# The output projection of an attention layer summed in PSUM by column blocks, most of it after the attention, with half a weight chunk per attention step

## The chip, the cores and the metric

The kernel runs on one core of a Trainium2 chip. The metric is device microseconds of one execution. TensorE (PE) multiplies, VectorE (DVE) and ScalarE (ACT) do everything elementwise, GpSimd (POOL) and SyncE (SP) start transfers. [...]

## The reference

One encoder layer on 256 tokens of width 2048: adaptive modulation from a condition vector `c`, windowed attention with a sink logit per head, and a squared-ReLU MLP. All in fp32.

```python
mod = silu(c) @ mod_w + mod_b                 # 2048 x 12288
sh_m, sc_m, g_m, sh_f, sc_f, g_f = split(mod, 6)
h = x * (1 + sc_m) + sh_m
q, k, v = split(h @ w_qkv + b_qkv)            # 32 query heads, 8 key heads of 64; rotary on q and k
m = max(max(s), sink);  p = exp(s - m);  p = p / (sum(p) + exp(sink - m))
y = (p @ v) @ w_o + b_o                       # 2048 x 2048
x = layer_norm(alpha * x + (1 + g_m) * y)
h = x * (1 + sc_f) + sh_f
y = square(relu(h @ w1 + b1)) @ w2 + b2       # 2048 x 8192 x 2048
x = layer_norm(alpha * x + (1 + g_f) * y)
```

## The kernel before

**Weights.** `Stream` loads every weight in chunks of 128x2048 fp32 (1 MB) on SP into one of five buffers `raw` (eight at the start). A matmul operand is split in two parts that the fast fp32 form of PE takes exactly: ACT writes the high part `wh` (L382), DVE the remainder `wl` (L351), each in halves of 128x1024, five buffers each. A product is three matmuls (`mm3`, L685 to L687): high by high, high by low, low by high. I call 12 such matmuls, all that one half of a chunk feeds for 256 tokens in the projections, a **half**; a chunk is two halves.

**Modulation.** A modulation chunk is computed in one of two ways. In the row form (`Mod.step`, L458) PE multiplies it by the condition vector; in the column form (`Col.step`, L498) DVE does, in one pass over 128x2048. The gate of the attention, `m_gm`, has eight chunks of the row form and eight of the column form (`GMP = 1`); the groups `m_ff[0]` and `m_ff[1]` for the MLP have four and four each (`FFP`). `Gate.spread` makes the gate vector a row for all partitions: PE transposes it, ACT copies it out (`grow`, L599), POOL writes it to memory (`rowm`, L600) and reads it back twice, once for each half of the columns, to all partitions (L602).

**Order.** The first part (to about 125 us) multiplies by most of w_qkv in an order that a planner makes. Seven chunks of w_qkv stay (`LATE`). Two of them run before the first scores. Then a loop over `n` interleaves 16 attention steps with one whole weight chunk a step: steps 0 to 4 take the last five chunks of w_qkv, and from `n = OUT_AT = 5` on there are 16 chunks of w_o, in the order of `OUTS`, four column blocks `c` for each of the four head groups `j`. Step `n` computes scores of four heads by 128 queries (`scores`: PE L922, then DVE L929 with mask and row minimum, then ACT L939 the exponential), `normalise` (DVE L947 and L951, ACT L954), and for the step before it the transposes of the probabilities (`probs_T`, PE L964, ACT L966); every second step `values` (PE L980) makes the attention output of a head pair, split into `oh` (ACT L983) and `ol` (DVE L984), which `project` multiplies by w_o.

**Sums of the projection.** `project(c, j)` adds up one head group in two PSUM banks and DVE adds them to a sum `ys` in SBUF (L1075 for `j = 0`, with the bias `bo` that a transfer spread over all partitions, and L1077). For `j = 3` `add_gated` (L989 to L991) multiplies by the gate, adds to the residual and takes statistics.

**Who decides the order.** The program names a sequence; a scheduler orders each engine's instructions ahead of time by its own estimate of when an operand is ready, and each engine then runs its list strictly in order. A wait of one instruction therefore holds up everything behind it on its engine. Modulation chunks stand in the stream in front of the weight chunk of their step (`SLOT_FILL` says how many).

After the projection come layer norm, the first MLP part (`W1A`, L1238 to L1240, with the rest of the modulation), and 620 us of dense MLP matmuls (L1264, L1266).

Of the kernel before, what the change touches and what calls it, by code (L numbers as in the profile page):

```python
# [15 lines left out]
OP = mybir.AluOpType  # L16
# [3 lines left out]
D = 2048  # L20
S = 256
NT = S // 128
NK = D // 128
# [27 lines left out]
def mod_chunks():  # L51

    out = []
    for which, sizes, prods in (("m", MIXG, MIXP), ("f", FFG, FFP)):
        k0 = 0
        for nk, p in zip(sizes, prods):
            out += [("w" + which, p, k0, i) for i in range(2 * p)]
            out += [("c" + which, n, k, 0) for k in range(k0 + p, k0 + nk) for n in range(2)]
            k0 += nk
    for which, p in (("m", GMP), ("f", 0)):  # L60
        out += [("rg" + which, h, i, 0) for h in range(p) for i in range(8)]
        out += [("cg" + which, 0, k, 0) for k in range(8 * p, NK)]
    return {c: i for i, c in enumerate(out)}
# [105 lines left out]
def hybrid_kernel(ctx: ExitStack, tc: tile.TileContext, a, out: bass.AP):  # L169
# [9 lines left out]
    def bank(name="pa"):  # L179
        return psum.tile([128, 512], F32, name=name, tag="bank")  # L180
# [92 lines left out]
    def bias_rows(src, n):  # L273
# [16 lines left out]

        def add(ps, c):
            nc.tensor.matmul(ps, sel[:, c * 128:c * 128 + 128], hl, start=False, stop=True)

# [271 lines left out]
    class Gate(Group):  # L565

        def __init__(self, which, p, gb):
            self.row = dram.tile([1, D], F32, name="row" + which)
            rows, cols, self.p, self.gb = [], [], p, gb
            self.ms = []  # L570
            for h in range(p):
                m = Mod([MODS["rg" + which, h, i, 0] for i in range(8)], 256)
                m.out = lambda m=m, h=h: self.rows(m, h)
                self.ms.append(m)
                rows += [(m, i) for i in range(8)]
            self.col = cst.tile([128, NK], F32, name="col" + which)
            cols = [(Col(MODS["cg" + which, 0, k, 0], self.col[:, k:k + 1]), 0)
                    for k in range(8 * p, NK)]
            self.set(rows, cols)

        def rows(self, m, h):
            pt = bank("pt")
            r = sml.tile([128, 256], F32, name="mrow", bufs=1)
            nc.scalar.copy(r, m.ps[:, :256])
            for x in range(2):
                nc.tensor.transpose(pt[:, x * 128:x * 128 + 128], r[:, x * 128:x * 128 + 128], ident)
            v = pt[:, :256].rearrange("p (x j q) -> p j x q", x=2, j=4)[:, :, :, 0]
            d = self.col[:, 8 * h:8 * h + 8].rearrange("p (j x) -> p j x", j=4)
            b = self.gb[:, 8 * h:8 * h + 8].rearrange("p (j x) -> p j x", j=4)
            nc.vector.tensor_tensor(d, v, b, op=OP.add)  # L590

        def spread(self, g):

            d, b = self.col[:, 8 * self.p:], self.gb[:, 8 * self.p:]
            nc.vector.tensor_tensor(d, d, b, op=OP.add)
# [85 lines left out]
    def part(tiles, t, c):  # L681
        return tiles[c][:, t * 512:t * 512 + 512]
# [302 lines left out]

    def add_gated(ps, t, c, gt, stats):
# [35 lines left out]
    def normed(c, t):  # L1022
# [8 lines left out]
        else:  # L1031
            tc.keep_in_program_order(nc.vector.tensor_scalar(z, z, mv[:, 0:1], rstd, op0=OP.subtract, op1=OP.mult))

    def project(c, j):

        pss = [bank() for _ in range(NT)]
        last = j == 3 and c == 3
# [3 lines left out]
        def step(t, rs):  # L1041
            for r in rs:
                s = slice(t * 512 + r * 128, t * 512 + r * 128 + 128)
                mm3(pss[t], oh[:, s], ol[:, s], wh(r), wl(r), r == 0, r == 3)

        if last:
            for t in range(NT):
# [3 lines left out]
                else:  # L1051
# [4 lines left out]
                    S.pump(4)  # L1056
                add_gated(pss[t], t, c, g1, st)
                sc.append(norm_scalars(st[t]))
# [5 lines left out]
        for r in (0, 2):  # L1064
            for t in range(NT):
                step(t, (r, r + 1))
            S.done()
            if r == 0:
                yield
        for t, ps in enumerate(pss):  # L1070
            if j == 0 and t == 0:
                ys[c] = g4b()
            y = part(ys, t, c)
            if j == 0:
                nc.vector.tensor_add(y, ps, bo(c))  # L1075
            elif j < 3:
                nc.vector.tensor_add(y, y, ps)  # L1077
            else:
                add_gated(ps, t, c, g1, st)
        if j == 2:  # L1080
            project_0(c)


    def project_0(c):

        for t in range(NT):
            y, z = part(ys, t, c), part(xs, t, c)
            nc.vector.tensor_mul(y, y, g1(c))
            nc.vector.scalar_tensor_tensor(z, z, ALPHA, y, op0=OP.mult, op1=OP.add)

# [20 lines left out]
    def mids(n):  # L1111
# [5 lines left out]
        return out  # L1117

    todo = []
    S.behind = True  # L1120
    for n in range(OUT_AT + 16):
        j, i = n // 4, n % 4
# [8 lines left out]
        w = iter(())  # L1131
        if n + PRE < len(LATE):
            w = qkv(*LATE[n + PRE])
        elif n >= OUT_AT:
            if n == OUT_AT:
                bo = bias_all(a["bo"], [g4b(), g4b()])
            w = project(*OUTS[n - OUT_AT])
        mid = mids(n)
        if j < 3:
# [16 lines left out]
        if n == 17:  # L1156
            ff_columns(0)


# [251 lines left out]
def _layout(i):  # L1411
# [13 lines left out]
    def chunk(kind, p, k, j):  # L1425
# [6 lines left out]
        if kind[0] == "r":  # L1432
            m = mw[:, g][:, p * 1024:p * 1024 + 1024].reshape(8, 2, 128, 1024)[k]
            return m.transpose(1, 0, 2).reshape(128, 2048)
# [55 lines left out]
```

## Time and profile before

| | us |
|---|---|
| median of 3 runs (lowest, highest) | 1085.61 (1085.3, 1085.9) |
| span of the profiled execution | 1083.7 |
| first scores on PE start | 165.06 |
| last projection matmul starts | 349.16 |
| DMA read and written | 291.68 MB |

The span runs from the first instruction to the last; what lies around it is 1.9 us against the median. The profile gives busy time per engine, groups of equal instructions with their mean duration and the idle time in front of them, timelines, and waits with the instruction that ended them. The start of an instruction is exact; rows of the same engine overlap slightly at their ends, so the distance of two starts is the price of a row in a dense stretch.

### The profile page before, as it was taken

The page shows a single profiled execution, that of the slowest core. Times are in us where ns is not written, and L with a number is a line of the kernel's source. Part 1 is how long each engine was busy: PE and PEld are TensorE (multiplying, and loading weights), DVE is VectorE, ACT ScalarE, POOL GpSimd, SP SyncE. Part 2 cuts the span into 40 slices and gives each one's busy share as a digit, 9 for nine tenths or more (in the row PEclk, how much of TensorE's full clock was granted, in tenths as well). Part 3 has the DMA queues.
Part 4 walks back from the last instruction along what each step waited for, and adds up shares of the span by engine and source line. Part 5 has one row for each costly group of instructions (what it writes and reads, how often), then busy time and mean ns, then how long its engine had stood idle before and what let it go on. Part 6 is the DMA issues. An engine that isn't in the chain of part 4 may idle for free.

```text
span 1083.7 us, 16256 instructions
## 1 busy us (share of the span) xinstructions
PE 1064.7 (98%) x6519; PEld 881.5 (81%) x6519; DVE 785.3 (72%) x1134; ACT 527.5 (49%) x814; POOL 19.7 (2%) x41
## 2 busy tenths in 40 slices
PE   8999999999999999999999999999999999999997
PEld 6777776677777899988888888888888888888885
DVE  3587689798799888754688789656665557665795
ACT  2453348777772646633345443344553334554340
POOL 2000000000000000000000010000000000000000
PEclk9999999999999999999999999999999999999999
DMA  9999997898973997555777889756555555557522
GB/s 380 425 425 425 427 407 270 352 348 344 391 277 122 420 352 273 193 194 194 272 272 274 295 293 319 297 203 222 194 194 188 192 193 201 181 181 263 194 78 78
DMA packets 43692, 292.75 MB, mean 270 GB/s; under 512 B 4916, under 2 KB 5076, under 8 KB 9824
## 3 DMA queue, kind: packets, MB, share of 16 engines
q1 hardware_dynamic: 40256, 281.82, 69.3%
q0 software_dynamic: 2496, 8.43, 2.3%
q10 hardware_dynamic: 864, 1.45, 0.4%
q8 instruction: 51, 0.84, 0.3%
q14 instruction: 25, 0.20, 0.0%
HBM read 289.57 MB, written 2.11 MB: 269 GB/s over the span
## 4 chain that ended last, share of the span: by engine, by line
PE 91%; DVE 5%; DMA 1%; ACT 1%; issue 1%; SPq 0%; DVEq 0%; ACTq 0%
PE pa L685 17%; PE pa L687 17%; PE pa L686 16%; PE pa L1264 16%; PE pa L1266 8%; PE pa L1240 3%; PE pa L1238 3%; PE pa L1239 3%; DVE raw L498 2%; PE pm L458 2%; PE gv L458 1%; PE pa L922 1%; PE pt L964 1%; PE pa L980 1%; DMA raw<-in_mod 1%; DVE wl L351 1%
## 5 line engine op out<-in xcount | busy, mean ns | idle before, releaser
L351 DVE TENSOR_TENSOR wl<-raw,wh 128x1024 fp32r<-128x1024 f32 x332 | 403.7, 1222 | 222.4 <-ACT wh L382 205.6
L382 ACT CAST wh<-raw 128x1024 fp32r<-128x1024 f32 x298 | 311.6, 1052 | 346.3 <-PE pa L687 203.1
L685 PE MATMUL pa<-wh,g 128*128 128x512 f32 x816 | 324.1, 398 | 2.7 <-ACT g L782 1.4
L687 PE MATMUL pa<-wh,g 128*128 128x512 f32 x816 | 319.3, 391 | 0.5 <-DVE g L984 0.4
L686 PE MATMUL pa<-wl,g 128*128 128x512 f32 x816 | 319.0, 391 | 0.5 <-DVE wl L351 0.4
L1264 PE MATMUL pa<-g,wh 128*128 128x512 f32 x768 | 192.3, 392 | 0.0
L685 PEld LDWEIGHTS pa<-wh,g 128*128 128x128 f32 x816 | 153.3, 188 | 42.7 <-issue 8.2
L687 PEld LDWEIGHTS pa<-wh,g 128*128 128x128 f32 x816 | 153.3, 188 | 34.6 <-issue 1.3
L686 PEld LDWEIGHTS pa<-wl,g 128*128 128x128 f32 x816 | 153.5, 188 | 31.4 <-DVE wl L351 1.2
L1264 PEld LDWEIGHTS pa<-g,wh 128*128 128x128 f32 x768 | 138.3, 189 | 25.1 <-ACT wh L382 0.2
L498 DVE CUSTOM_DVE_ANT_0 raw<-raw,cb 128x2048 f32<-128x2048 f32 x52 | 118.5, 2283 | 9.3 <-ACT cb L868 5.6
L1266 PEld LDWEIGHTS pa<-g,wl 128*128 128x128 f32 x768 | 104.8, 190 | 7.5
L1266 PE MATMUL pa<-g,wl 128*128 128x256 f32 x768 | 107.1, 282 | 0.0
L1240 PE MATMUL pa<-g,wl 128*128 128x256 f32 x256 | 72.3, 284 | 1.9 <-DVE wl L351 1.9
L1238 PE MATMUL pa<-g,wh 128*128 128x256 f32 x256 | 72.7, 285 | 0.3 <-ACT g L1173 0.3
L1239 PE MATMUL pa<-g,wh 128*128 128x256 f32 x256 | 72.4, 284 | 0.0
L1240 PEld LDWEIGHTS pa<-g,wl 128*128 128x128 f32 x256 | 48.9, 192 | 2.1 <-DVE wl L351 2.1
L1238 PEld LDWEIGHTS pa<-g,wh 128*128 128x128 f32 x256 | 49.1, 192 | 1.0 <-ACT g L1173 0.6
L1239 PEld LDWEIGHTS pa<-g,wh 128*128 128x128 f32 x256 | 49.1, 192 | 0.4 <-issue 0.4
L393 ACT CAST wh<-raw 128x1024 fp32r<-128x1024 f32 x34 | 34.8, 1048 | 21.8 <-DMA raw<-in_wqkv 19.6
L939 ACT ACTIVATE g<-g,nm 128x256 f32<-128x256 f32 x64 | 31.8, 498 | 13.1 <-DVE nm L929 13.0
L929 DVE CUSTOM_DVE_ANT_0 g<-pa,msk,nsnk 128x256 f32<-128x256 f32 x64 | 27.1, 477 | 6.3 <-PE pa L922 6.3
(204 smaller groups left out, 743.6 us busy)
## 6 DMA issues: line engine op xcount, KB each, us to landing
raw<-in_mod SPq DMA_DIRECT2D x96, 1024.0 KB, 8.8
raw<-in_w SPq DMA_DIRECT2D x64, 1024.0 KB, 4.8
raw<-in_w1b SPq DMA_DIRECT2D x48, 1024.0 KB, 4.8
raw<-in_wqkv SPq DMA_DIRECT2D x24, 1024.0 KB, 15.3
raw<-in_wo SPq DMA_DIRECT2D x16, 1024.0 KB, 7.4
raw<-in_w1a SPq DMA_DIRECT2D x16, 1024.0 KB, 7.4
g<-in_x SPq DMA_DIRECT2D x4, 512.0 KB, 9.1
gb<-in_lnrow POOLq DMA_DIRECT2D x8, 256.0 KB, 5.7
```

Of the source, the lines that this page charges most:

```text
L351: self.pinned(nc.vector.tensor_sub(l, r, f32(self.hs[n])))
L382: self.last[n] = nc.scalar.copy(h, s)
L393: self.pinned(nc.scalar.copy(h, s))
L498: S.pinned(nc.vector.tensor_tensor_reduce(out=raw, in0=raw, in1=cb, scale=1.0, scalar=0.0, op0=OP.mult, op1=OP.add, accum_out=self.dst))
L685: S.pinned(nc.tensor.matmul(ps, xh, wh, start=start, stop=False))
L686: nc.tensor.matmul(ps, xh, wl, start=False, stop=False)
L687: S.prev = nc.tensor.matmul(ps, xl, wh, start=False, stop=stop).ins
L1238: nc.tensor.matmul(o, wh(w, 128), hh, start=new, stop=False)
L1239: nc.tensor.matmul(o, wh(w, 128), hl, start=False, stop=False)
L1240: nc.tensor.matmul(o, wl(w, 128), hh, start=False, stop=end)
L1264: nc.tensor.matmul(ps, wh(k, 128), ff_in(k), start=k == 0, stop=False)
L1266: nc.tensor.matmul(ps[:, :256], wl(k, 128), ff_in(k)[:, :256], start=False, stop=k == NK - 1)
```

## The change

The modulation: `m_gm` gets twelve chunks of the row form and four of the column form (`GMP = 3`, with rows of four chunks in place of eight), `m_ff[0]` and `m_ff[1]` get eight of the column form each and none of the row form. The bytes are the same.

The weights beside the attention: `HALVES` says how many halves a step takes. Attention steps 0 to 16 take one each, step 8 two; the twelve steps behind take two each. `chain` is the one sequence of halves that the steps draw from, so the order of chunks is by sequence, not by step number. Modulation is planned one chunk a step up to the thirteenth step, then none for three steps, and two a step behind the attention.

The projection: the chunks go by column block (`OUTS`), and the two banks of a block stay open over all four head groups (`out_of`). The bias comes as one more matmul a bank (`bo`, through `bias_rows` as for qkv). The sums `ys` in SBUF, the additions and `project_0` go; `add_gated` takes the factor alpha of the residual into its second operation. The gate is spread after step 15 in place of step 11.

```diff
-OUT_AT = 5
-X_AT = 11
-SLOT_FILL = (1, 1, 1, 1, 1, 1, 1, 2, 2, 2, 2, 2, 2, 2, 2, 2, 2, 2, 2, 2, 1, 0, 0)
+HALVES = (2, 2, 1, 1, 1, 1, 1, 1, 1, 1, 2, 1, 1, 1, 1, 1, 1, 1, 1, 2, 2, 2, 2, 2, 2, 2, 2, 2, 2, 2, 2)
+X_AT = 12
+SLOT_FILL = (1, 1, 1, 1, 1, 1, 1, 1, 1, 1, 1, 1, 1, 1, 1, 1, 0, 0, 0, 1, 2, 2, 2, 2, 2, 2, 2, 2, 1, 0, 0)
-FFP = (2, 2, 4, 0)
-GMP = 1
+FFP = (0, 0, 4, 0)
+GMP = 3
...
-    OUTS = [(c, j) for j in range(4) for c in range(4)]
-    for n in range(-PRE, OUT_AT + 16):
+    OUTS = [(0, 0), (0, 1), (0, 2), (1, 0), (0, 3), (1, 1), (1, 2), (1, 3), (2, 0), (2, 1), (2, 2), (2, 3), (3, 0), (3, 1), (3, 2), (3, 3)]
+    halves = taken = 0
+    for n in range(-PRE, len(HALVES) - PRE):
         plan_late(SLOT_FILL[n + PRE])
...
-        if n + PRE < len(LATE):
-            wq(*LATE[n + PRE])
-        elif n >= OUT_AT:
-            S.plan(a["wo"][OUTS[n - OUT_AT]])
+        halves += HALVES[n + PRE]
+        while 2 * taken < halves:
+            v = (LATE + OUTS)[taken]
+            if taken < len(LATE):
+                wq(*v)
+            else:
+                S.plan(a["wo"][v])
+            taken += 1
...
-        nc.vector.tensor_add(z, z, tmp)
+        if scale is None:
+            nc.vector.tensor_add(z, z, tmp)
+        else:
+            nc.vector.scalar_tensor_tensor(z, z, scale, tmp, op0=OP.mult, op1=OP.add)
...
-        pss = [bank() for _ in range(NT)]
+        pss = out_of[c] = out_of.get(c) or banks()
...
-                mm3(pss[t], oh[:, s], ol[:, s], wh(r), wl(r), r == 0, r == 3)
+                mm3(pss[t], oh[:, s], ol[:, s], wh(r), wl(r), j == 0 and r == 0, j == 3 and r == 3)
...
+            if r and j == 0:
+                for t in range(NT):
+                    bo(pss[t], c, False)
...
-        for t, ps in enumerate(pss):
-            if j == 0 and t == 0:
-                ys[c] = g4b()
-            y = part(ys, t, c)
-            if j == 0:
-                nc.vector.tensor_add(y, ps, bo(c))
-            elif j < 3:
-                nc.vector.tensor_add(y, y, ps)
-            else:
-                add_gated(ps, t, c, g1, st)
-        if j == 2:
-            project_0(c)
+        if j == 3:
+            for t in range(NT):
+                add_gated(pss[t], t, c, g1, st, ALPHA)
...
+    def chain():
+        for v in LATE[PRE:]:
+            yield from qkv(*v)
+            yield
+        for v in OUTS:
+            yield from project(*v)
+            yield
...
-        next(w, None)
+        if k:
+            next(work)
+        else:
+            S.pump(2)
         for f in mid:
             f()
-        next(w, None)
+        if k > 1:
+            next(work)
...
-        if n == 11:
+        if n == 7:
+            split_bo, bo = bias_rows(a["bo"], D)
+        if n == 8:
+            split_bo()
+        if n == 15:
             g1 = m_gm.spread([g4(), g4()])
```

The change moves instructions on each engine. Three places show it; in all of them the rows are the lists of one engine, in the order in which it runs them. (Line numbers after the change are up to eleven higher: L498 and L351 stay, L884 to L891 of the rotary positions become L887 to L894, L929 becomes L932, L922 becomes L925, L964 becomes L967, L984 becomes L987, L989 becomes L992.)

DVE, from the second column-form chunk (`colm`, L498) to the first scores (`msk`), before. `trig` marks the rotary positions of a block of queries or keys, `wl` a weight remainder.

```order
L498 ISA raw,colm<-raw,cb 128x2048
L498 ISA colm 128x1
L886 TENSOR_TENSOR g_1463<-g_1354,trig 128x16x32
L889 TENSOR_TENSOR g_1354<-g_1354,trig 128x16x32 x2
L351 TENSOR_TENSOR wl<-raw,wh 128x1024
L891 TENSOR_TENSOR g_1354<-g_1354,g_1463 128x1024
L351 TENSOR_TENSOR wl<-raw,wh 128x1024
L929 ISA g_1545,nm<-pa,msk,nsnk 128x256
```

The same stretch of the changed kernel, from the end of the same rotation on:

```order
L894 TENSOR_TENSOR g_1354<-g_1354,g_1495 128x1024
L351 TENSOR_TENSOR wl<-raw,wh 128x1024 x2
L498 ISA raw,colm<-raw,cb 128x2048
L498 ISA colm 128x1
L787 TENSOR_TENSOR g_657<-g_657,pa 128x512 x2
L889 TENSOR_TENSOR g4b<-g_657,trig 128x16x32 x2
L892 TENSOR_TENSOR g_657<-g_657,trig 128x16x32 x2
L588 TENSOR_TENSOR colm<-pt,pack 128x4
L894 TENSOR_TENSOR g_657<-g_657,g4b 128x1024
L351 TENSOR_TENSOR wl<-raw,wh 128x1024
L498 ISA raw,colm<-raw,cb 128x2048
L932 ISA g_1595,nm<-pa,msk,nsnk 128x256
```

Two more column-form chunks, the addition of a finished qkv block, its whole rotation and one `wl` now stand between that rotation and the first scores.

PE, the changed kernel, from the end of the third late w_qkv chunk. `pt<-ident,g` are transposes, first of the keys and queries (L910), then of the probabilities of step 0 (L967); L925 are the scores of steps 0 and 1, then of 2.

```order
L690 MATMUL pa<-wh,g_1115 128x512
L292 MATMUL pa<-g_127,g_129 128x512 x2
L458 MATMUL pm<-raw,cact 32x128 x16
L585 MATMUL pt<-ident,mrow 128x128
L910 MATMUL pt<-ident,g_1343 128x128 x8
L910 MATMUL pt<-ident,g_1354 128x128 x8
L925 MATMUL pa<-g_1545,g_1576 128x256 x8
L458 MATMUL pm<-raw,cact 32x128 x16
L967 MATMUL pt<-ident,g_1595 128x128 x8
L925 MATMUL pa<-g_1545,g_1576 128x256 x4
L688 MATMUL pa<-wh,g_255 128x512
```

Before, the scores of step 0 stood inside the third late chunk, with seven of its matmuls, the bias and the scores of step 1, and then 15 matmuls of the fourth behind them and ahead of the transposes of step 0; now that chunk stands ahead of the key transposes, and one modulation chunk is all that lies between the scores and the transposes.

DVE, the changed kernel, behind the last scores. L992 is the first operation with the spread gate (`g_2865`); L987 makes the low part `g_2790` of the last `values`.

```order
L351 TENSOR_TENSOR wl<-raw,wh 128x1024
L498 ISA raw,modf<-raw,cb 128x2048
L498 ISA modf 128x1
L992 TENSOR_TENSOR tmp<-pa,g_2865 128x512
L987 TENSOR_TENSOR g_2790<-pa,g_2789 128x512
L996 SCALAR_TENSOR_TENSOR g_2110<-g_2110,tmp 128x512
L498 ISA raw,modf<-raw,cb 128x2048
```

On PE the first user of that low part stands 19 rows behind the last transposes' first row, in the projection of head group 3:

```order
L983 MATMUL pa<-g_2900,g_1365 64x256 x4
L689 MATMUL pa<-wl,g_2154 128x512
L690 MATMUL pa<-wh,g_2155 128x512
L688 MATMUL pa<-wh,g_2154 128x512
L689 MATMUL pa<-wl,g_2154 128x512
L688 MATMUL pa<-wh,g_2789 128x512
L689 MATMUL pa<-wl,g_2789 128x512
L690 MATMUL pa<-wh,g_2155 128x512
L688 MATMUL pa<-wh,g_2154 128x512
L690 MATMUL pa<-wh,g_2790 128x512
```

Before, the first operation with the gate came some 20 us behind the copy `grow`, and the low parts of `values` had no gate operation ahead of them.

More of the change, by code (lines that the diff above doesn't have):

```diff
@@ L60, in mod_chunks @@
     for which, p in (("m", GMP), ("f", 0)):
-        out += [("rg" + which, h, i, 0) for h in range(p) for i in range(8)]
-        out += [("cg" + which, 0, k, 0) for k in range(8 * p, NK)]
+        out += [("rg" + which, h, i, 0) for h in range(p) for i in range(4)]
+        out += [("cg" + which, 0, k, 0) for k in range(4 * p, NK)]
     return {c: i for i, c in enumerate(out)}
@@ L289, in split, with add @@
             nc.scalar.copy(sel, one)
-        def add(ps, c):
-            nc.tensor.matmul(ps, sel[:, c * 128:c * 128 + 128], hl, start=False, stop=True)
+        def add(ps, c, stop=True):
+            nc.tensor.matmul(ps, sel[:, c * 128:c * 128 + 128], hl, start=False, stop=stop)
         return split, add
@@ L571, in __init__ @@
             for h in range(p):
-                m = Mod([MODS["rg" + which, h, i, 0] for i in range(8)], 256)
+                m = Mod([MODS["rg" + which, h, i, 0] for i in range(4)], 128)
                 m.out = lambda m=m, h=h: self.rows(m, h)
                 self.ms.append(m)
-                rows += [(m, i) for i in range(8)]
+                rows += [(m, i) for i in range(4)]
             self.col = cst.tile([128, NK], F32, name="col" + which)
             cols = [(Col(MODS["cg" + which, 0, k, 0], self.col[:, k:k + 1]), 0)
-                    for k in range(8 * p, NK)]
+                    for k in range(4 * p, NK)]
             self.set(rows, cols)
@@ L583, in rows @@
             r = sml.tile([128, 256], F32, name="mrow", bufs=1)
[L584 to L589, printed above, removed]
+            nc.scalar.copy(r[:, :128], m.ps[:, :128])
+            nc.tensor.transpose(pt[:, :128], r[:, :128], ident)
+            v = pt[:, :128].rearrange("p (j q) -> p j q", j=4)[:, :, 0]
+            d, b = (u[:, 4 * h:4 * h + 4] for u in (self.col, self.gb))
             nc.vector.tensor_tensor(d, v, b, op=OP.add)
         def spread(self, g):
-            d, b = self.col[:, 8 * self.p:], self.gb[:, 8 * self.p:]
+            d, b = self.col[:, 4 * self.p:], self.gb[:, 4 * self.p:]
             nc.vector.tensor_tensor(d, d, b, op=OP.add)
@@ L984, in values, with add_gated @@
         return lambda: nc.vector.tensor_sub(ol, po, f32(oh))
-    def add_gated(ps, t, c, gt, stats):
+    def add_gated(ps, t, c, gt, stats, scale=None):
         tmp = sml.tile([128, 512], F32, name="tmp", tag="t2", bufs=3)
@@ L1032, in normed @@
             tc.keep_in_program_order(nc.vector.tensor_scalar(z, z, mv[:, 0:1], rstd, op0=OP.subtract, op1=OP.mult))
+    out_of = {}
     def project(c, j):
-        pss = [bank() for _ in range(NT)]
+        pss = out_of[c] = out_of.get(c) or banks()
         last = j == 3 and c == 3
@@ L1056, in project @@
                     S.pump(4)
-                add_gated(pss[t], t, c, g1, st)
+                add_gated(pss[t], t, c, g1, st, ALPHA)
                 sc.append(norm_scalars(st[t]))
@@ L1069, in project @@
                 yield
-        for t, ps in enumerate(pss):
-            if j == 0 and t == 0:
-                ys[c] = g4b()
-            y = part(ys, t, c)
-            if j == 0:
-                nc.vector.tensor_add(y, ps, bo(c))
-            elif j < 3:
-                nc.vector.tensor_add(y, y, ps)
-            else:
-                add_gated(ps, t, c, g1, st)
-        if j == 2:
-            project_0(c)
[L1084 to L1089, printed above, removed]
+        if j == 3:
+            for t in range(NT):
+                add_gated(pss[t], t, c, g1, st, ALPHA)
     a2 = cst.tile([128, NK], F32, name="a2")
@@ L1117, in mids @@
         return out
+    def chain():
[5 more added lines that the diff above has]
+            yield
     todo = []
+    work = chain()
     S.behind = True
-    for n in range(OUT_AT + 16):
+    S.pace = 1
+    for n in range(len(HALVES) - PRE):
         j, i = n // 4, n % 4
@@ L1130, in hybrid_kernel @@
             late_tiles.append(1)
[L1131 to L1137, printed above, removed]
+        k = HALVES[n + PRE]
         mid = mids(n)
@@ L1432, in chunk @@
         if kind[0] == "r":
-            m = mw[:, g][:, p * 1024:p * 1024 + 1024].reshape(8, 2, 128, 1024)[k]
+            m = mw[:, g][:, p * 512:p * 512 + 512].reshape(4, 4, 128, 512)[k]
             return m.transpose(1, 0, 2).reshape(128, 2048)
```

3 lines of the change are left out of this document (2 added, 1 removed).

## The prediction, made before the changed kernel ran

> **What bounds the kernel now.** I read the page's first part, then a table of windows around the attention, then PE's waits, then timelines.
>
> ```profile
> span 1083.7 us, 16256 instructions
> ...
> PE 1064.7 (98%) x6519; PEld 881.5 (81%) x6519; DVE 785.3 (72%) x1134; ACT 527.5 (49%) x814; POOL 19.7 (2%) x41
> ```
>
> PE is busy for 1064.7 of 1083.7 us. So time goes down only if PE has less to do or waits less, and only 19 us of waiting exist in the whole span. The part that the change touches lies between 120 and 350 us:
>
> ```profile
> core 0: us, PE busy (x) PEld busy (x) DVE busy (x) ACT busy (x) POOL busy (x), PEclk, DMA share, GB/s
> ...
> 120.00:165.00 45.00, 44.49 (x287) 33.70 (x287) 36.44 (x43) 18.31 (x26) 0.64 (x2) 1.00 0.94 393
> 165.00:312.00 147.00, 146.25 (x1083) 105.46 (x1083) 127.43 (x277) 112.05 (x275) 3.15 (x6) 1.00 0.91 347
> 312.00:350.00 38.00, 38.00 (x204) 29.84 (x206) 34.76 (x64) 15.70 (x30) 0.00 (x0) 1.00 0.43 153
> ```
>
> The columns are the stretch, then the busy time of PE, its weight loads, DVE, ACT and POOL, the granted clock, the DMA share and the rate. PE stands still for 0.5, 0.75 and 0.0 us in these three stretches, at full clock. DVE is the next engine (127 of 147 us). The waits of PE in the stretch from 120 to 361 us say which are left:
>
> ```profile
> PE pt L1167 <- ACT g L1030: 1.4, 1, 1.4
> ...
> PE pa L687 <- DVE g L984: 0.4, 1, 0.4
> ...
> PE pt L964 <- ACT g L954: 0.3, 1, 0.3
> ```
>
> The largest (1.4) belongs to the layer norm, which stays. The softmax wait (L964 for the normalised probabilities) costs 0.3 us, once: between scores and transposes PE has enough dense matmuls. The change takes half of these matmuls away from the attention, so what it can gain on PE must stand against waits that are hidden now.
>
> **The change part by part.** The PE prices are distances of starts:
>
> ```profile
> 139.53 0.62 PE L292 MATMUL pa<-g,g 128*128 128x512 f32 x2
> 139.99 0.39 PE L685 MATMUL pa<-wh,g 128*128 128x512 f32 x1
> 140.22 0.39 PE L686 MATMUL pa<-wl,g 128*128 128x512 f32 x1
> ...
> 155.38 1.04 PE L907 MATMUL pt<-ident,g 128*128 128x128 f32 x8
> ...
> 162.73 1.07 PE L458 MATMUL pm<-raw,cact 128*32 128x256 f32 x16
> 163.73 1.09 PE L907 MATMUL pt<-ident,g 128*128 128x128 f32 x8
> ...
> 173.41 0.84 PE L964 MATMUL pt<-ident,g 128*128 128x128 f32 x4 [0.27 <-ACT g L954]
> ```
>
> A dense matmul costs 0.23, a half 12 x 0.227 = 2.72, a pair of bias matmuls 0.46, a row-form modulation chunk 1.0 to 1.1, eight transposes 0.8 to 1.05.
>
> *PE's work.* The row form goes from 8 + 4 + 4 to 12 chunks in these three groups: 4 fewer, -4.4 us. The bias adds eight matmuls, +1.8. One transpose of the modulation goes, -0.1. Sum **-2.7** (-3.2 to -2.2). The two small waits above vanish or are counted below in another form: **-0.7**.
>
> *DVE's work.* Out go 16 additions to `ys`, eight with the bias and sixteen of `project_0`, each under 0.7 us, some 24 us; in come four column-form chunks, 8.8 us.
>
> ```profile
> L382 ACT CAST wh<-raw 128x1024 fp32r<-128x1024 f32 x49 | 50.8, 1048 | 20.4 <-PE pa L687 20.0 <-DMA raw<-in_wqkv 0.2
> ...
> L1077 DVE TENSOR_TENSOR g4b<-g4b,pa 128x512 f32<-128x512 f32 x16 | 10.9, 681 | 3.5 <-PE pa L687 3.5
> ```
>
> I cost this relief at nothing. It lies on an engine that PE never waited for longer than 0.4 us here. Where DVE stands does matter, and that is the next term.
>
> *The first softmax.* Up to 160.58 us DVE's list is the same before and after, so the trace of before gives the start, and prices for what follows:
>
> ```profile
> 146.57 1.29 DVE L889 TENSOR_TENSOR g<-g,trig 128x512 f32<-128x512 f32 x2
> 147.78 1.22 DVE L351 TENSOR_TENSOR wl<-raw,wh 128x1024 fp32r<-128x1024 f32 x1
> ...
> 153.09 1.28 DVE L784 TENSOR_TENSOR g<-g,pa 128x512 f32<-128x512 f32 x2
> ...
> 156.56 2.28 DVE L498 CUSTOM_DVE_ANT_0 raw<-raw,cb 128x2048 f32<-128x2048 f32 x1
> 158.77 0.08 DVE L498 DVE_READ_ACCUMULATOR2_ANT colm<- 128x1 f32 x1
> ...
> 160.58 1.22 DVE L351 TENSOR_TENSOR wl<-raw,wh 128x1024 fp32r<-128x1024 f32 x1
> 161.72 1.22 DVE L891 TENSOR_TENSOR g<-g,g 128x1024 f32<-128x1024 f32 x1
> 162.85 1.22 DVE L351 TENSOR_TENSOR wl<-raw,wh 128x1024 fp32r<-128x1024 f32 x1
> ...
> 166.34 0.48 DVE L929 CUSTOM_DVE_ANT_0 g<-pa,msk,nsnk 128x256 f32<-128x256 f32 x1 [2.27 <-PE pa L922]
> ...
> 167.96 1.22 DVE L351 TENSOR_TENSOR wl<-raw,wh 128x1024 fp32r<-128x1024 f32 x1
> ```
>
> A column-form chunk costs 2.2, a `wl` 1.14, a rotated block 1.13, a pair of 128x512 operations 1.2, four score rows 1.62. Before, DVE was idle for 2.27 us when the first scores came: it was early. Now DVE runs from 160.58: rotation 161.7, two `wl` 164.0, column form 166.2, and the addition pair (its PE sums end with the bias at about 165.2) 167.4, two rotation pairs 169.8, the small one 169.9, last rotation 171.0, `wl` 172.2, column form 174.4. Only then come the scores of step 0, until 176.0; those of step 1 and a `wl` stand ahead of the sum that the normalisation needs, 179.2.
>
> ```profile
> 172.85 1.71 ACT L954 ACTIVATE g<-g,rs 128x256 f32<-128x256 f32 x4 [1.03 <-DVE rs L951]
> ```
>
> ACT normalises until 180.9 and the eight transposes end at about 181.6. PE meanwhile: 36 matmuls, a bias pair and two modulation chunks from 155.38 bring it to 166.3; the transposes of `mrow`, keys and queries to 169.2, scores of steps 0 and 1 to 171.4, one modulation chunk to 172.5. Its next rows are the transposes of step 0, and everything dense stands behind them. It could end them at 173.6 and ends them at 181.6: **+8.0** (7 to 9).
>
> *The clock behind a wait.* After a long wait of PE the trace shows a lower granted clock:
>
> ```profile
> 14.94 1.08 PE L458 MATMUL gv<-raw,cact 128*32 128x128 f32 x32 [2.03 <-DMA raw<-in_mod]
> ...
> 16.00:18.00 2.00, 2.00 (x9) 1.42 (x6) 0.16 (x1) 0.00 (x0) 0.00 (x0) 0.62 1.02 418
> 18.00:20.00 2.00, 2.00 (x34) 1.38 (x32) 0.00 (x0) 0.00 (x0) 0.00 (x0) 0.53 1.02 422
> ```
>
> Two windows at 0.62 and 0.53 lose 0.76 + 0.94 = 1.7 us. I take **+1.7** after the first softmax (0 if the clock holds, 3.4 if it falls twice). [...]
>
> *The later attention steps.* Beside them PE loses 15 halves (17 in place of 32) and about six modulation chunks: 146.25 - 41 - 6 = 99 us. ACT loses 15 `wh` of 1.0: 112.05 - 15 = 97. So PE and ACT now have nearly equal work, and the chain from scores over softmax to transposes gets half the cover that it had. PE takes one score group ahead, so most of the chain should hide; I take **+2** of 0 to 10. The upper end is 16 steps with some 0.6 us each uncovered; the row of 0.3 above is nearer to the low end.
>
> *The gate row.* `Gate.spread` moves from step 11 to step 15, and DVE's first use of it (L992) now stands ahead of L987, whose low part PE needs 19 rows behind the last transposes. From the copy `grow` PE has about 34 dense matmuls, eight transposes and eight `values` matmuls to do, 7.7 + 0.8 + 1.0, less the 0.5 of the copy: about 9 us until it needs L987. How long the row takes is shown twice, beside weight loads and in the MLP:
>
> ```profile
> 280.87 0.25 ACT L599 COPY grow<-pt 16x128 f32<-16x128 f32 x1
> ...
> 286.82 1.08 POOL L602 DMA_DIRECT2D g<-rowm  x2 [4.91 <-DMA rowm<-grow]
> ...
> DMA to landing us min/median/max: 5.1/10.0/13.2
> ```
>
> ```profile
> 731.08 0.24 ACT L599 COPY grow<-pt 16x128 f32<-16x128 f32 x1
> ...
> 734.46 1.08 POOL L602 DMA_DIRECT2D g4b<-rowf  x2 [2.34 <-DMA rowf<-grow]
> ...
> DMA to landing us min/median/max: 2.6/4.0/6.3
> ```
>
> The first half of the row lands 286.82 + 10.0 - 281.12 = 15.7 us behind the copy in the first case, and 734.46 + 4.0 - 731.32 = 7.1 in the second. With L992 and L987 (0.6 each) L987 ends 8.3 to 16.9 us behind the copy: a wait of 0 to 8. Around step 15 the changed kernel plans no modulation for three steps and half a chunk of weights a step, so I take the middle, **+4**. [...] The clock behind this wait: **+1** (0 to 1.7).
>
> *Behind the attention* 26 halves of 2.72 us follow. The window from 312 to 350 shows this kind of work without any idle time on PE and with DMA at 0.43. DVE has less to add there than before, so I cost it at nothing. So with the transfers of the bias: two small ones several steps ahead of their first use.
>
> The sum: -2.7 - 0.7 + 8.0 + 1.7 + 2 + 4 + 1 = +13.3. On the span of 1083.7 this is 1097.0; the median of the runs, 1085.61, is 1.9 above the span, so **1099**.
>
> **Rivals.** *The gate row lands in time.* PE comes later than I think, or the transfers are as short as in the MLP. Terms of 4 and 1 go: 1094. For it: only half of the earlier load stands in the queue. Against: the row beside weight loads, 15.7.
>
> *The attention loop becomes bound by ACT and DVE in turn.* For it: 99 against 97 us of work and a chain of five engine changes a step. Against: four score rows, exponential and normalisation of different steps can overlap. The term of the later steps becomes 10: 1107.
>
> *The PE saving decides.* If DVE reaches the first scores by about 168 in place of 174, since PE's modulation chunk and the score groups of two steps cover the softmax from there on, no long wait arises, the later steps stay covered and the gate row lands in time: 1083.7 - 3.4 + 1.9 = 1082, faster. The point is DVE's place in its list: the two extra column-form chunks and the rotation make 9 us of it, and the list cannot be passed by. It would need these chunks to be much cheaper than 2.2 us, for which no row speaks.
>
> *The change does not do what it says.* If the projection still ran beside the attention, cover would stay. The lists speak against it: of the 32 halves of w_o eight stand beside the steps.
>
> **How the numbers follow.** Chances: both waits as summed 0.50 (1095 to 1104); the gate row in time 0.21 (1094); the loop bound by its chain 0.16 (1107); the saving decides 0.07 (1082); a balance of saving and smaller waits within 0.2% 0.06. About 0.2% is what a measurement of this kernel can tell from no change. So faster 0.07, same 0.06, slower 0.87. The range from 1088 to 1110 leaves out the fast case and the far end of the chain case.
>
> **What would show it.** In the new profile PE must show one wait of 7 to 9 us at the first transposes of the probabilities (L967), released by ACT's normalisation, with DVE's first score row (L932) near 174 and no idle time ahead of it. A second wait must stand at an L690 for L987, whose own DVE wait is for the transfer of `rowm`. PE's busy time must be near 1062. If DVE waits for PE at its first scores, the largest term is wrong; if L992 does not wait, that one; if PE waits at every L967, it is the chain.

## The result and the profile after

| | before | changed |
|---|---|---|
| median (lowest to highest, runs), us | 1085.76 (1085.3 to 1086.61, 4) | 1103.89 (1099.74 to 1104.98, 4) |
| ratio, 95% interval | | 1.0159 (1.014 to 1.0178) |
| span of the profiled execution, us | 1083.7 | 1103.2 |

The changed kernel is slower by 1.6%. Two executions far outside the others (4221 us of run 7's kernel, the one that was profiled, and 1508 us of the kernel before beside run 11) have no part in any ratio here. The page of the changed kernel begins:

```profile
span 1103.2 us, 16263 instructions
...
PE 1070.4 (97%) x6526; PEld 887.9 (80%) x6526; DVE 772.3 (70%) x1104; ACT 527.3 (48%) x815; POOL 22.8 (2%) x45
```

The span grew by 19.5 us. PE is busy for 5.7 us more, although it was given less to do (time at a lower clock counts as busy: the window from 182 to 184 below shows 2.00 us of 2 at a clock of 0.50), and idle for 13.8 us more. DVE is busy for 13 us less: the relief came, on the engine that does not set the end. PE's timeline shows that all of the loss lies ahead of the layer norm: the long run of modulation chunks behind the last projection matmul started at 349.48 and starts 19.58 later, and the first MLP matmul (356.10 before, 375.68 now) is late by the same 19.58.

```profile
349.48 3.66 PE L458 MATMUL pm<-raw,cact 128*32 128x256 f32 x64
```

```profile
369.06 3.66 PE L458 MATMUL pm<-raw,cact 128*32 128x256 f32 x64
```

(The first row is of before, the second of the changed kernel.) The waits of PE between 120 and 385 us in the changed kernel, with total, count and longest:

```profile
PE pt L967 <- ACT g L957: 8.1, 2, 7.8
PE pa L690 <- DVE g L987: 4.1, 1, 4.1
PE pt L1174 <- ACT g L1036: 1.4, 1, 1.4
PE pt L585 <- ACT mrow L584: 1.0, 2, 0.6
...
PE pt L910 <- issue: 0.7, 1, 0.7
```

The first two rows hold the waits of the prediction (the first row is the wait of 7.75 us and one of 0.34); the third is the old one of the layer norm. Up to the last projection matmul the changed kernel's waits sum to 13.4 us more than before.

**The first softmax**, in DVE's timeline and then PE's:

```profile
160.62 1.23 DVE L894 TENSOR_TENSOR g<-g,g 128x1024 f32<-128x1024 f32 x1
...
164.03 2.28 DVE L498 CUSTOM_DVE_ANT_0 raw<-raw,cb 128x2048 f32<-128x2048 f32 x1
...
172.36 2.28 DVE L498 CUSTOM_DVE_ANT_0 raw<-raw,cb 128x2048 f32<-128x2048 f32 x1
174.57 0.08 DVE L498 DVE_READ_ACCUMULATOR2_ANT colm<- 128x1 f32 x1
174.57 0.48 DVE L932 CUSTOM_DVE_ANT_0 g<-pa,msk,nsnk 128x256 f32<-128x256 f32 x1
```

```profile
171.23 1.08 PE L458 MATMUL pm<-raw,cact 128*32 128x128 f32 x32
180.07 2.16 PE L967 MATMUL pt<-ident,g 128*128 128x128 f32 x8 [7.75 <-ACT g L957]
```

`CUSTOM_DVE_ANT_0` is the profile's name for the kernel's `tensor_tensor_reduce` (the column form at L498, the scores at L932); its rows here measure 2.28 and 0.48 us. DVE's first score row starts at 174.57 with no idle time ahead of it, as forecast for 174.4; PE stands still for 7.75 us.

**The gate row**, on ACT, POOL, DVE and PE, and the landing times of the tile `rowm`:

```profile
290.30 0.24 ACT L597 COPY grow<-pt 16x128 f32<-16x128 f32 x1
```

```profile
296.20 1.08 POOL L600 DMA_DIRECT2D g<-rowm  x2 [4.87 <-DMA rowm<-grow]
...
DMA to landing us min/median/max: 4.8/6.2/6.9
```

```profile
302.50 0.69 DVE L992 TENSOR_TENSOR tmp<-pa,g 128x512 f32<-128x512 f32 x1 [6.94 <-DMA g<-rowm]
303.11 0.68 DVE L987 TENSOR_TENSOR g<-pa,g 128x512 fp32r<-128x512 f32 x1
```

```profile
303.85 0.80 PE L690 MATMUL pa<-wh,g 128*128 128x512 f32 x1 [4.07 <-DVE g L987]
```

The first half of the row lands 296.20 + 6.2 - 290.54 = 11.9 us behind the copy, near the middle of the two cases shown before (7.1 and 15.7). The DMA share over these 11.9 us is 0.87; over the 15.7 us of the loaded case before it is 0.99, over the 7.1 us in the MLP 0.59. DVE waits for it with the low part of `values` queued behind, and PE waits for that.

**The clock** falls in both waits and stays low behind them. In these windows the last three columns are granted clock, DMA share and rate:

```profile
176.00:178.00 2.00, 0.00 (x0) 0.00 (x0) 2.00 (x12) 2.00 (x10) 0.00 (x0) 0.50 0.84 328
...
180.00:182.00 2.00, 1.93 (x8) 1.35 (x8) 0.16 (x1) 2.00 (x8) 0.00 (x0) 0.50 1.00 348
182.00:184.00 2.00, 2.00 (x10) 1.18 (x8) 1.97 (x5) 2.00 (x4) 0.00 (x0) 0.50 0.85 324
184.00:186.00 2.00, 2.00 (x6) 1.49 (x5) 2.00 (x8) 2.00 (x7) 0.00 (x0) 0.50 0.23 98
...
302.00:304.00 2.00, 0.15 (x1) 0.16 (x1) 1.50 (x3) 0.00 (x0) 0.00 (x0) 0.56 0.43 176
304.00:306.00 2.00, 2.00 (x5) 1.61 (x6) 2.00 (x2) 0.04 (x1) 0.00 (x0) 0.50 0.04 8
306.00:308.00 2.00, 2.00 (x6) 1.52 (x6) 2.00 (x4) 1.00 (x1) 0.00 (x0) 0.50 0.44 57
308.00:310.00 2.00, 2.00 (x8) 1.59 (x7) 1.82 (x3) 1.05 (x1) 0.00 (x0) 0.73 0.79 311
```

Half speed lasts from 176 to 186 and from about 302 to 309. Counted from where PE works again, it costs some 3.1 us (0.97 + 1 + 1, and 0.1 in the window from 186, which has 0.95) and 2.6 us (0.1 + 1 + 1 + 0.5). With 13.4 us of waits that makes 19.1 of the 19.6 us. What is left for PE's work, forecast at -2.7, is then about +0.5.

### The profile page after: what moved, and what is told of

The parts are those of the page before. It is cut to its first block, busy times and chain, and to the rows that moved or that the text cites. A ratio compares the mean times of both kernels' runs of the same rounds, so it can differ in the third digit from the quotient of the medians.

```text
span 1103.2 us, 16263 instructions
## 1 busy us (share of the span) xinstructions
PE 1070.4 (97%) x6526; PEld 887.9 (80%) x6526; DVE 772.3 (70%) x1104; ACT 527.3 (48%) x815; POOL 22.8 (2%) x45
## 4 chain that ended last, share of the span: by engine, by line
PE 88%; DVE 6%; DMA 3%; ACT 2%; issue 1%; SPq 0%; DVEq 0%; POOLq 0%; ACTq 0%
PE pa L688 16%; PE pa L690 16%; PE pa L689 16%; PE pa L1271 16%; PE pa L1273 8%; PE pa L1247 3%; PE pa L1245 3%; PE pa L1246 3%; DMA raw<-in_mod 2%; DVE raw L498 2%; PE gv L458 2%; PE pa L925 1%; PE pm L458 1%; PE pa L983 1%; PE pt L967 1%; DVE wl L351 1%
## 5 line engine op out<-in xcount | busy, mean ns | idle before, releaser
L351 DVE TENSOR_TENSOR wl<-raw,wh 128x1024 fp32r<-128x1024 f32 x332 | 403.5, 1222 | 225.7 <-ACT wh L382 210.4
L498 DVE CUSTOM_DVE_ANT_0 raw<-raw,cb 128x2048 f32<-128x2048 f32 x56 | 127.7, 2285 | 12.8 <-DMA raw<-in_mod 7.1
L393 ACT CAST wh<-raw 128x1024 fp32r<-128x1024 f32 x34 | 34.7, 1048 | 19.1 <-DMA raw<-in_wqkv 16.9
L942 ACT ACTIVATE g<-g,nm 128x256 f32<-128x256 f32 x64 | 31.7, 497 | 10.2 <-DVE nm L932 9.6
L932 DVE CUSTOM_DVE_ANT_0 g<-pa,msk,nsnk 128x256 f32<-128x256 f32 x64 | 27.2, 479 | 8.3 <-PE pa L925 8.3
```

The costliest lines, as they stand in the source:

```text
L351: self.pinned(nc.vector.tensor_sub(l, r, f32(self.hs[n])))
L393: self.pinned(nc.scalar.copy(h, s))
L498: S.pinned(nc.vector.tensor_tensor_reduce(out=raw, in0=raw, in1=cb, scale=1.0, scalar=0.0, op0=OP.mult, op1=OP.add, accum_out=self.dst))
```

## The experiments

**1. The modulation alone, on the kernel before.**

```diff
-FFP = (2, 2, 4, 0)
-GMP = 1
+FFP = (0, 0, 4, 0)
+GMP = 3
...
-                m = Mod([MODS["rg" + which, h, i, 0] for i in range(8)], 256)
+                m = Mod([MODS["rg" + which, h, i, 0] for i in range(4)], 128)
```

> The kernel before with the modulation of the change alone (m_gm twelve row-form and four column-form chunks, m_ff[0] and m_ff[1] all column form); projection, sums and one whole weight chunk a step as before. Theory (the loss comes from waits that lost their cover, not from the form of the modulation): PE loses four row-form chunks, 4 x 1.05 us, and a transpose, waits stay as before, so 4 us less than before (3 to 5). Rival (more modulation on VectorE makes the first softmax late): a wait of 4 us or more at the first transposes of the probabilities, and no gain or a loss.

Measured: 1089.24 us, ratio 1.0031 (1.0021 to 1.0041). Neither came whole. There is a small loss, as the rival has it, but the first softmax has no wait, so the rival's cause falls. PE waits at another place, for a rotation on DVE:

```profile
265.01 2.28 DVE L498 CUSTOM_DVE_ANT_0 raw<-raw,cb 128x2048 f32<-128x2048 f32 x1
...
267.23 2.28 DVE L498 CUSTOM_DVE_ANT_0 raw<-raw,cb 128x2048 f32<-128x2048 f32 x1
...
269.51 1.21 DVE L889 TENSOR_TENSOR g4b<-g4b 128x1024 f32<-128x1024 f32 x1
```

```profile
270.78 1.97 PE L905 MATMUL pt<-ident,g4b 128*128 128x128 f32 x8 [5.27 <-DVE g4b L889]
```

Two column-form chunks, 4.4 us, stand directly ahead of the last addition of the rotation that the query transposes need. Run 11 issues that addition earlier, and the wait goes.

**2. The projection alone**, with the modulation of before (`FFP = (2, 2, 4, 0)`, `GMP = 1` and its row form in the changed kernel).

> The changed kernel with the modulation of before (eight row-form and eight column-form chunks of m_gm, four and four of m_ff[0] and m_ff[1]); projection and half a chunk a step as changed. Theory (half a chunk a step takes the cover): five dense matmuls, one modulation chunk and a bias pair, some 2.7 us, are left between the first scores and their transposes, so PE waits 3 to 5 us there, and 3 to 5 us for the last values behind the gate row, each with 2 to 3 us of lower clock: 12 to 16 us over before (ratio 1.011 to 1.015). Rival (the column form causes the first wait): no wait there, at most 8 us over before.

Measured: 1100.59 us beside 1086.76 for before on that chip, ratio 1.013 (1.0115 to 1.0145). PE's waits:

```profile
PE pt L969 <- ACT g L959: 3.1, 1, 3.1
PE pa L692 <- DVE g L989: 2.8, 1, 2.8
```

The total is as expected, the second wait a little under the 3 to 5 us. Both waits are there without the new modulation, and this run makes 13.8 of the changed kernel's 18.1 us. DVE is not late here: with one column-form chunk ahead of the scores in place of two, and no second rotation, it waits 0.41 us for PE at its first score row (166.52). So the first wait is 3.1 us even where DVE comes to the scores in time; the rest of the 7.75 goes with DVE's longer list.

**3. Cover at the first softmax.** One half is moved from step 8 to step 0.

```diff
-HALVES = (2, 2, 1, 1, 1, 1, 1, 1, 1, 1, 2, 1, ...
+HALVES = (2, 2, 2, 1, 1, 1, 1, 1, 1, 1, 1, 1, ...
```

> The changed kernel with one number moved: step 0 takes two halves in place of one, step 8 one in place of two. 25 dense matmuls then stand between the first scores and their transposes. Theory: the first wait (7.75 us in the changed kernel) falls to under 1 us and the 3 us of lower clock behind it go too: 9 to 11 us less than the changed kernel; the gate wait of 4.1 us stays. Rival (VectorE is too late anyway, and the wait moves to the second transposes): a wait of 4 us or more at one of the next transposes, and less than 5 us gained.

Measured: 1094.24 us, 9.7 less than the changed kernel's 1103.89, ratio to before 1.0075 (1.0059 to 1.0092). The size is as expected, and no transpose of the first softmax waits. That the size fits is luck, because the sum is of other parts: the gate wait, expected to stay, went too, and three smaller ones came.

```profile
PE pt L585 <- ACT mrow L584: 2.1, 2, 1.6
PE pt L967 <- ACT g L957: 1.9, 1, 1.9
...
PE pa L925 <- DVE g L987: 1.3, 1, 1.3
```

The gate wait went because the low part now happens to stand ahead of the gate operation on DVE:

```profile
293.84 0.69 DVE L987 TENSOR_TENSOR g<-pa,g 128x512 fp32r<-128x512 f32 x1 [2.54 <-ACT g L986]
294.45 0.68 DVE L992 TENSOR_TENSOR tmp<-pa,g 128x512 f32<-128x512 f32 x1
```

One moved half reorders the lists behind that place, so this run shows that cover removes the first wait; it does not price that wait by itself.

**4. The low part ahead of the gate operation**, by an ordering edge; from 120 us up to that place DVE's list keeps its order.

```diff
-        return lambda: nc.vector.tensor_sub(ol, po, f32(oh))
+        return lambda: lows.append(nc.vector.tensor_sub(ol, po, f32(oh)))
...
+            tc.add_manual_dep(i.ins, lows[-1].ins.name, ORDER_ONLY, reason="behind")
```

> The changed kernel with VectorE's order held at one place: the first operation with the gate row stands behind the low part of the last values (an ordering edge without a semaphore). Theory: PE's wait of 4.07 us for that low part goes with the 2.4 us of lower clock behind it: 6 to 7 us less than the changed kernel. Rival (the gate row then holds up the weight remainders behind it): PE waits 3 us or more for a wl a few matmuls later, and under 2 us are gained.

Measured: 1098.35 us, 5.5 less than the changed kernel, ratio to before 1.0109 (1.0092 to 1.0126). DVE's rows (L994 is the gate operation):

```profile
298.11 0.69 DVE L987 TENSOR_TENSOR g<-pa,g 128x512 fp32r<-128x512 f32 x1
...
302.45 0.69 DVE L994 TENSOR_TENSOR tmp<-pa,g 128x512 f32<-128x512 f32 x1 [0.85 <-DMA g<-rowm]
```

The row lands when it did; only PE's need for it is gone, and the remainders behind the gate operation are not late. In the profiles the first MLP matmul comes at 369.02 in place of 375.68, 6.66 earlier, about the 4.07 of wait and 2.6 of clock (0.3 of it was there before, from a shorter stretch of half speed at the first wait). The span is only 5.1 shorter, since in this profile the clock falls once more behind the layer norm (368 to 374), which costs 1.7 us; that may be why the median gains a little less than the 6 to 7 us expected. The first wait is 7.75 as before. This is the cleanest of the runs.

**5. Modulation chunks moved away from the first scores**, with the edge of run 4.

```diff
-SLOT_FILL = (1, 1, 1, 1, 1, 1, 1, 1, 1, 1, 1, 1, 1, 1, 1, 1, 0, ...
+SLOT_FILL = (2, 2, 0, 0, 0, 1, 1, 1, 1, 1, 1, 1, 1, 1, 2, 1, 0, ...
```

> The changed kernel with the ordering edge of the run before (low part of the last values ahead of the first gate operation), and the modulation chunks of its plan moved: two each at the two late chunks ahead of step 0, none at steps 0 to 2, so that no column-form chunk stands between the second rotation and the first scores and 18 or more dense matmuls between these scores and their transposes. Theory: both waits (7.75 and 4.07 us) and the lower clock behind them (3.0 and 2.4) go: 15 to 18 us less than the changed kernel, within 2 us of the kernel before. Rival (PE and ACT have equal work beside the attention, and the waits come back at other steps): over 3 us in sum of PE waits at transposes or values, and 5 us or more over before.

Measured: 1097.74 us, ratio 1.0107 (1.0091 to 1.0124): the theory missed by some 10 us. The rival's size came, but only 0.9 us of wait is at `values` and none over 0.2 us at a transpose of the attention. Both waits are gone, but PE now waits for ACT's copy of a finished modulation row:

```profile
239.48 0.33 PE L585 MATMUL pt<-ident,mrow 128*128 128x128 f32 x1 [3.71 <-ACT mrow L584]
```

That copy stands on ACT behind four exponentials (237.20 to 239.19), which waited for DVE's scores. In all PE's waits up to the first MLP matmul are 8.5 us longer than before, and the clock falls once more (at 240). Taking the two waits away in this way is not enough. That ACT and DVE have no slack beside the attention fits this, but one arrangement does not show it.

**6 to 11: can the modulation's saving be kept on the kernel before?** In run 1 the wait for the rotation hides it. Five variants (run 9 is run 7's kernel once more) ask whether place or number of the column-form chunks costs.

Run 6: run 1 with its plan thinned at steps 7 to 10 (`SLOT_FILL` one in place of two, the rest behind the attention).

> The modulation of the change alone on the kernel before, as in the first run, with its plan of chunks thinned: one a step instead of two at steps 7 to 10, the four that are left behind the attention. Theory (the wait of 5.27 us for the rotation of the last head group comes from pairs of column-form chunks ahead of it on VectorE, and hides a PE saving of 4 us): that wait falls under 1 us, its lower clock goes, and the time is 3 to 5 us below before (ratio 0.995 to 0.997). Rival (VectorE is full through the attention, and the delay only moves): a PE wait of 3 us or more for VectorE at another place, and no gain over before.

Measured: 1098.2 us, ratio 1.0114 (1.0099 to 1.0129). Missed: the rotation wait is still 3.7 us, and a load of a row-form chunk comes late. There is no gain, as the rival has it, but the new long wait is for a load and not for VectorE.

```profile
PE pm L458 <- DMA raw<-in_mod: 4.9, 2, 4.2
PE pt L905 <- DVE g4b L889: 3.7, 1, 3.7
```

Run 7: the four chunks in `m_ff[1]` alone, so that they stand behind the last rotation (`FFP = (2, 0, 4, 0)`, all else as before).

> The kernel before with one number changed: m_ff[1] has all eight chunks in column form (four row-form chunks fewer on PE, four column-form chunks more on VectorE: the same two amounts as in the first run), and these chunks stand behind the rotation of the last head group. Theory (what costs is the place of a column-form chunk, ahead of something that PE waits for, not their number): no new wait over 1 us, PE's four chunks of 1.05 us are kept: 3 to 4.5 us below before (ratio 0.996 to 0.997). Rival (VectorE is full, any four chunks more make PE wait): a new PE wait of 3 us or more for VectorE, no gain.

Measured: 1088.27 us, ratio 1.0019 (1.001 to 1.0027). No gain: missed.

Run 8: two row-form chunks fewer (`FFP = (2, 1, 4, 0)`).

> The same with two row-form chunks fewer in m_ff[1] in place of four. Theory: half the gain of the run before, 1.5 to 2.5 us below before. Rival: as there.

Measured: 1083.38 us, ratio 0.9974 (0.9962 to 0.9986): 2.5 us faster than before, as expected in size. Beside the attention PE has one new wait over 0.1 us, for a load, which the theory did not have; the profiled execution (1085.38 us) was one of the two slowest of the six:

```profile
301.82 1.07 PE L458 MATMUL pm<-raw,cact 128*32 128x256 f32 x16 [1.94 <-DMA raw<-in_mod]
```

Run 9: run 7's kernel once more.

> The kernel before with all of m_ff[1] in column form once more, for its profile. Theory: the first 265 us show no new wait (the lists are the same up to the last rotation); behind it two column-form chunks a step keep their buffers so long that the load of a row-form chunk comes late, and PE waits 3 to 6 us for such loads (transfer of in_mod), as the run with two chunks fewer does for 1.94 us. Rival: PE waits for VectorE (a remainder or a sum), not for a load.

Measured (one execution): 1087.4 us. Two waits for loads of in_mod, 0.77 and 0.88 us, less than expected, and one of 1.13 us for a remainder on DVE near 346 us; no new wait for VectorE ahead of that. The waits of the theory are there but too small to keep the gain away. The lower clock takes 1.7 us more than in the profile of before (a second drop, 404 to 408); the rest is open.

Run 10: run 8 with `SLOT_FILL` one in place of two at two late steps (13 and 14) and the two chunks behind the attention; the third place that the expectation names keeps its number.

> The kernel before with two row-form chunks fewer in m_ff[1], as two runs before, and its plan of chunks thinned at three steps near the end of the attention (one instead of two at steps 13 and 14 and at step 18 two lines on, the rest behind). Theory: the wait of 1.94 us for a load of in_mod goes, and the time falls by 1.5 to 2 us more, 3.5 to 4.5 us below before (ratio 0.996 to 0.997). Rival: the wait moves behind the attention, ratio 0.997 to 1.0 as before it.

Measured: 1085.78 us, ratio 1.0001 (0.9991 to 1.001). The load wait is gone and the gain too: the rival's ratio. Its wait behind the attention is hardly there (1.67 us at the layer norm in place of 1.39). In the profile the clock falls twice, which costs 1.7 us more than in run 8 or before; why the other executions gain nothing is not shown.

Run 11: run 1 with the last addition of each rotation issued one step earlier.

```diff
                 mid += [lambda: next(turn), lambda: next(turn)]
-            if i == 2:
                 mid.append(lambda: qA.__setitem__(j + 1, next(turn)))
```

> The modulation of the change alone on the kernel before, as in the first run, with the last addition of a rotation issued one attention step earlier. Theory: the wait of 5.27 us for the rotation of the last head group goes with 2.6 us of lower clock; nothing else differs from the first run, so some 8 us less than that, 3.5 to 5 us below before (ratio 0.9955 to 0.997). Rival (VectorE is full, the delay moves on to the sums or the remainders): a PE wait of 3 us or more for VectorE or for a load of in_mod behind that place, ratio 1.0 or more.

Measured: 1090.58 us, ratio 1.0039 (1.0025 to 1.0052). The rotation wait is gone, as the theory says, and nothing is won, as the rival says, though its 3 us are spread over two waits:

```profile
PE pm L458 <- DMA raw<-in_mod: 3.3, 2, 2.6
```

PE waits for loads instead. That column-form chunks which DVE reaches late hold the five load buffers fits this, but was not tried by itself.

**12. Run 8 once more.**

> The kernel with two row-form chunks fewer in m_ff[1] on the kernel before once more, on whichever chip this falls. Theory: the PE saving of two chunks (2.1 us) less one wait of 1.94 us for a load is nothing; what was measured before as 2.5 us came from a period of lower clock that did not occur in that profile near 14 us; so the ratio lies between 0.997 and 1.0, and the single times stand in groups some 1.7 us apart. Rival (the gain is real work saved): 0.996 to 0.9985 again, without such groups.

Measured: 1084.18 us, ratio 0.9984 (0.9975 to 0.9994). With run 8 it is faster than both kernels of this study, by 0.16 to 0.26%, the best that was found. The rival fits better than the theory: the load wait did not occur in this profile, and the times spread from 1083.2 to 1087.8 without clear groups. The clock does not explain the gain either. It costs 1.7 us in each of the three profiles, before (16 to 20), run 8 (402 to 408) and here (352 to 358), and yet the span here, 1081.7, is 2.0 below the 1083.7 of before: about the work of two row-form chunks (2.1). In run 8's profile the load wait of 1.94 us took that back.

## Why the prediction was right, point by point

- **PE's work, -2.7.** This term was mis-sized, and its sign was wrong: the remainder after waits and clock is about +0.5. Its saving came nearly as said, the price of the bias did not. The groups of the modulation chunks (L458) in PE's table, before and changed, from 120 us to the first MLP matmul, and the rows of bias (L292) and `values` (L980 and L983):

```profile
L458 PE MATMUL pm<-raw,cact 128*32 128x128 f32 (+1 forms) x480 | 23.0, 326 | 0.0
...
L980 PE MATMUL pa<-g,g 128*64 128x256 f32 x128 | 15.6, 385 | 0.0
...
L292 PE MATMUL pa<-g,g 128*128 128x512 f32 x12 | 3.7, 389 | 0.0
```

```profile
L458 PE MATMUL pm<-raw,cact 128*32 128x128 f32 (+1 forms) x480 | 18.8, 297 | 0.0
L983 PE MATMUL pa<-g,g 128*64 128x256 f32 x128 | 17.5, 389 | 0.0
L292 PE MATMUL pa<-g,g 128*128 128x512 f32 x20 | 6.3, 395 | 0.0
```

  Modulation -4.2 (forecast -4.4) and bias +2.6 (forecast +1.8: busy for about 0.66 a pair in place of 0.46). What the sum left out is that `values`, equal in number, are busy for 1.9 us more. Before, each group of sixteen matmuls stood together; now most stand apart in smaller pieces. Two pieces of eight are busy for 2.16 us (1.08 each at 296.66) in place of 1.95 (188.79 before); by the start of the row behind them it is 2.02 in place of 1.88, so the busy time overstates it. No run changes this alone. The scores are busy for 2.1 us more (20.2 against 18.1) and the transposes of the probabilities for 0.9 more (19.1 against 18.2), but eight of each stand in the stretch of half speed behind the first wait (0.63 us in place of 0.40 a score, 0.42 in place of 0.28 a transpose), which is most of it. PE's busy time, which the prediction gave as a sign, came to 1070.4 in place of near 1062: besides this term, that figure leaves out the time at lower clock, which counts as busy and which the sum did have.
- **Small waits, -0.7, and the later steps, +2.** Five waits of 0.3 to 0.7 us (mrow twice, an attention copy, one for issue, one softmax) sum to 2.3; the two old ones are gone. Two of the five (0.39 and 0.34) stand ahead of the first softmax, so the later steps have 1.6 of them. Right within the range. PE and ACT run side by side, and the chain shows only in such pieces.
- **The first softmax, +8.0.** 7.75 at the place, by the rows and with the cause named. Run 3 shows that cover removes it, run 2 that it comes without the new modulation, shorter where DVE's list is shorter, and run 1 that the new modulation under the old cover brings none here.
- **The gate row, +4.** 4.07. Run 4 removes it by order alone, with the row landing as late as before: the late row costs PE something only because L992 stands in front of L987.
- **The clock, +1.7 and +1.** 3.1 and 2.6. The direction was right, the size was taken from a wait of 2.03 us with 3.4 us of half speed; after the longer waits half speed lasted 10.2 and 6.8 us, part of it while PE still waited. No length of wait fits all drops: PE stopped at 172.3 and the clock fell at 176.0, 3.7 us later; in the second wait it fell after only 2.5 us (299.8 to about 302.3); and drops came behind waits of 1.4 and 2.0 us, shown at the end.
- **The transfers.** The row landed 11.9 us behind the copy at a DMA share of 0.87, nearer to the 0.99 of the loaded case than to the 0.59 of the MLP. The reason for taking the middle, half the earlier load, thus held only in small part, and that +4 came out at 4.07 is partly luck. It took longer than the 7.1 us of the MLP; the loaded case of 15.7 did not come.

The sum of +13.3 was 6 us short of 19.5: some 3 in PE's work and 3 in the clock. The waits, forecast at 13.3 in sum, came to 13.4. So the mechanism was right, and the measured 1103.89 stands at the upper edge of the 1095 to 1104 that went with it. The rival of a bound attention loop gave nearly the same time as was measured, but for another reason: at the later steps the waits are small.

## What to carry to other kernels

Where PE is 98% busy, count what covers each softmax before moving matmuls away from it: one modulation chunk (1.1 us) in place of the old stretch, with a longer list on DVE, cost 7.75 us of wait here. In a fixed order, an instruction that waits for a transfer must not stand ahead of one that the bounding engine needs; one ordering edge was worth 5.5 us of the time, 6.7 at the end of the attention part. A saving of a few microseconds of PE work was easily lost to waits elsewhere: of six ways to keep 2 to 4 us of modulation (runs 1, 6, 7, 8, 10 and 11), one, run 8, kept about 2.

## What the hardware showed that was not expected

In the profiles of this case the lower clock costs 1.7 us or about a multiple of it, called portions here, and the length of a wait alone does not tell whether one follows. Summed over windows of 2 us up to the end of PE's work, the loss in a profile is 1.70 us before, 1.72 in run 8, 1.70 in run 12, 3.4 in runs 5, 9, 10 and 11, 5.1 in runs 1 and 2, 6.8 in run 3, 8.5 in run 4, 10.2 in run 6 and 10.3 in the changed kernel: one, two, three, four, five and six portions. In the changed kernel one lies behind the load near 15 us, three at the first softmax and two at the gate row; of the last five, 2.0 and 0.8 us fall into PE's waits and cost nothing beside them. Before, a wait of 2.03 us at 14.94 was followed by 0.62 and 0.53 (1.7 us); in run 8 a wait of 2.06 us at the same place was not:

```profile
14.55 1.08 PE L458 MATMUL gv<-raw,cact 128*32 128x128 f32 x32 [2.06 <-DMA raw<-in_mod]
```

```profile
16.00:18.00 2.00, 2.00 (x38) 1.47 (x36) 0.00 (x0) 0.00 (x0) 0.00 (x0) 1.00 1.08 444
18.00:20.00 2.00, 2.00 (x19) 1.58 (x10) 0.03 (x1) 0.27 (x1) 0.00 (x0) 1.00 0.97 397
```

But run 8 lost its portion behind another wait, of 1.93 us for a remainder, which left the clock at 1.00 before (402 to 408 in both; in run 8 the three windows have 0.77, 0.50 and 0.87):

```profile
404.00:406.00 2.00, 2.00 (x11) 2.00 (x10) 1.90 (x7) 0.00 (x0) 0.00 (x0) 0.50 1.04 414
```

The layer-norm wait of 1.39 to 1.40 us left the clock at 1.00 before and in the changed kernel; in runs 4 and 12 a portion follows it, and in run 3 the same wait was followed by

```profile
366.00:368.00 2.00, 2.00 (x17) 0.78 (x10) 1.60 (x5) 1.88 (x5) 0.00 (x0) 0.50 1.02 430
368.00:370.00 2.00, 2.00 (x13) 1.96 (x12) 1.80 (x4) 2.00 (x4) 0.00 (x0) 0.69 1.03 434
```

that is 1.0 + 0.6 and 0.1 in the window ahead of them, again 1.7 us. At a clock of 0.50 a loss of 1.7 us stands for 3.4 us of time, an estimate from these windows. Why the loss comes in such portions, and why a wait of 1.4 us is followed by one in some profiles and not in others, was not shown. So two profiles of kernels with such waits can differ by 1.7 us without a cause that shows in their waits: 1.7 of the 3.2 us between the spans of runs 10 and 12, but none of the 1.9 between runs 8 and 12, which lost the same.
